# The gate ahead of the prompt's attention in a hybrid decoder layer: score banks, a pool for probabilities, and the planned order

## The chip, the core and the metric

The kernel runs on one core of one Trainium2 chip. It is one launch; what counts is device time in microseconds (us), the median of several executions. The core has a matrix engine (TensorE, PE in the rows), three engines for elementwise work (VectorE or DVE, ScalarE or ACT, GpSimd or POOL), a queue on SyncE (SP) that issues every transfer of this kernel, an on-chip memory of 128 partitions (SBUF) and eight accumulator banks (PSUM) into which TensorE writes. Each engine works through its own list of instructions in order and waits for the others by semaphores.

## What is computed

One inference step of one decoder layer, for a prompt of 512 tokens and for eight samples of one token with 2,048 tokens of past each, which lie in pages of 128 tokens. The part of the reference around which the change works, shortened:

```python
kc = _compress(ck, pk, w1k, w2k); vc = _compress(cv, pv, w1v, w2v)   # gelu(blocks @ w1) @ w2
s = einsum('bqgrd,bkgd->bgrqk', q, kc) * ATTN_SCALE                   # compressed branch
p = _masked_softmax(s, cmp_end <= q_pos); o_c = einsum(p, vc)
...                                                                   # importance -> top 16 blocks
s = einsum('bqgrd,bgqnd->bgrqn', q_rot, ks) * ATTN_SCALE              # selected branch
p = _masked_softmax(s, kmask); o_s = einsum(p, vs)
s = einsum('bqgrd,bkgd->bgrqk', q_rot, kw) * ATTN_SCALE               # window branch
p = _masked_softmax(s, wm); o_w = einsum(p, vw)
o = gate0 * o_c + gate1 * o_s + gate2 * o_w
...
s = einsum('bqhmd,bkhmd->bhmqk', qb, dk) * ATTN_SCALE                 # differential attention
p = softmax(where(k_pos <= q_pos, s, -inf)); o = einsum(p, dv)
o = rmsnorm(o[..., 0, :] - lam * o[..., 1, :], subln_g)
```

The same is done for the prompt (all keys are its own) and for each sample (keys from the pages). Then come the output projection, a gated feed-forward network with a short convolution, and the last norm.

## The kernel before, in words

The program has four parts in time: the input projection (to about 180 us), the compression of the samples' pages (to about 320 us), attention (to about 480 us), and the output projection and the feed-forward network (to the end). From the projection on to the first products of the output projection, the order is not written by hand. Small generators (`p_...`) yield one operation at a time with the events (`E(...)`) that it needs and sets; class `Issue` plays them against each other with planned times, picks the next one for each engine and emits the instructions in that order. The kernel is built 69 times: eight rehearsals, each planned from the latest starts of the one before it, then 60 variants with random shifts of the best plan, and last the build with the plan that ended first. So a change to one generator can move instructions anywhere in this part, and a time that the planner reckons with is not a time of the chip.

The generators that matter here:

- `p_product` multiplies the split pages of sample `b` with the compression's weights `w1`, first the keys (`k`), then the values (`v`): 24 products (three for each of eight steps) for each of 32 units in `cunits`. The sums of one sample and kind share a bank of `ACC`, a ring of four banks; `p_post` takes it from there (gelu, then the products named `hy,w2p` for keys and `w2v,hy` for values).
- `p_scores` and `p_window` collect the sample's scores against the selected pages and the window in banks 6 and 7 (`Ss`, `Sw`; products `cp,Qzs` and `qu,Qzs`).
- `p_nsa(b2)` (L1563) is the softmax of those scores for four samples. VectorE finds maxima, TensorE transposes them (`cst,nsc`, L1584), VectorE reduces, TensorE transposes back (`cst,m`, L1597), VectorE copies, ScalarE does three exponentials, VectorE adds, TensorE sums (`nsc,cst`), VectorE takes the reciprocal and scales `Ss`, TensorE transposes it (`cst,Ss`, L1628) and `Sw` (`cst,Sw`, L1639).
- `p_v` is the sample's product of probabilities with the pages of values: `vp,Sd` and `vp,Ss`, two pages for each load, eight and four matmuls. `p_vload` issues the 64 loads into a ring `VS` of six buffers. A buffer comes free after the `vp,Ss` of its pair of loads.
- `p_qk(i)` is the score step of unit `i` of the prompt (12 units: 4 heads' rows times the branches selected, window and differential). In the order each unit makes three packs for each of two groups: query blocks 0 and 1 (128 and 256 keys), block 2 (384) and block 3 (512), named `z,q` or `z,dq`. A pack needs a bank of `SR`, a ring of four. `p_exp` empties it: VectorE's masked minimum (L1835, `CUSTOM_DVE_ANT_0` in the rows), then ScalarE's exponential into a tile `p0` to `p3`. `p_scale` divides by the sums, `p_turn` transposes the probabilities (L1896), `p_pv` multiplies with the values.
- `p_switch` closes the pools of the compression: the event `right` comes when the pages are split and scored and the last key products are done, and opens the pools `W0` and `VR` (for the vp loads); `left` comes when everything that uses pool `C1` is done, and opens pool `AT` (for the prompt's tiles).
- `p_main` (L2243) runs all units' `p_qk` in a row.

In the kernel before, `p_main` waits for `left`, for `Sw` and `Ss` to be out of their banks, and for the last accumulator of the values; the banks of the roles are fixed: scores in 0, 1, 7 and 2, outputs in 3.

Of the kernel before, what the change touches and what calls it, by code (L numbers as in the profile page):

```python
# [20 lines left out]
B = 8  # L21
# [208 lines left out]
class Slot:  # L230


    def __init__(self, ring):
        self.ring, self.got, self.done = ring, Event(), Event()
        n = len(ring.slots)
        self.needs = [ring.slots[n - ring.size].done] if n >= ring.size else []
        if n:
            self.needs.append(ring.slots[n - 1].got)
        ring.slots.append(self)


class Ring:
    def __init__(self, size):
        self.size, self.slots = size, []
# [176 lines left out]
def _build(tc, T, plan, last):  # L421
# [838 lines left out]
    def p_product():  # L1260
        yield E("w", 23)
        yield E("w", 24)
        for n, (b, kv, sh) in enumerate(cunits):
# [10 lines left out]
            for i in range(2):  # L1274
                wh, wl = w1[kv, i]
                for s in range(4):
# [11 lines left out]
                    sets = [asl] if first else []  # L1288
                    if (i, s) == (1, 3):
                        sets += [wsl.done, E("prod", n)]  # L1290
# [452 lines left out]
    def p_switch():  # L1743
# [6 lines left out]
        def f():  # L1750
            RAW[1].close()
            RAW[0].close()
            Q0.close()
            PL["W0"] = Pool(tc, "W0", side="right")
            PL["VR"] = Pool(tc, "VR", side="right")
            pcs.append(PL["W0"]("wo", [128, 1024], F32, 3).rearrange("p (a b) -> p a b", b=512))
# [65 lines left out]
    def p_exp(i, g, qs, box, sl, wslot):  # L1822
# [4 lines left out]
        for q in qs:  # L1827
# [4 lines left out]
            def f():  # L1832
                if q == 0 and g == 0:
                    W[i] = at("w", [128, 6, 4], F32, 4)
                ve.tensor_tensor_reduce(out=x, in0=x, in1=cm[:, S - n:], scale=-SC, scalar=3e38, op0=OP.add, op1=OP.min,  # L1835
                                        accum_out=W[i][:, g, q:q + 1])
            yield (("dve", tdve(n), f, PS),) + ((wslot,) if first and q == 0 else ())
        for q in qs:
# [4 lines left out]
            def f():  # L1843
                t = at(f"p{q}", [128, n], F32, NPR[q])
                act(t, xs[q], AF.Exp, bias=W[i][:, g, q:q + 1], scale=-1.0, accum_out=W[i][:, 2 + g, q:q + 1])
                PB[i, g, q] = t, pr
# [33 lines left out]
    def p_turn(i):  # L1880
        br, r, gs = units[i]
        for c in range(3):
# [242 lines left out]
    def p_half(b, vb, sl):  # L2125
# [3 lines left out]
        b2, b4 = b // 4, b % 4  # L2129

# [112 lines left out]
    def p_main():  # L2243
        for e in (E("left"), E("Sw"), E("Ss", 1)):
            yield e
        yield cacc["v", B - 1].done
# [5 lines left out]
        Q.spawn(p_out(2, 1, OR, "o"), 7, Q.now)  # L2252

# [11 lines left out]
    for f, prio in ((p_stage2(), 0), (p_load(), 0), (p_w1v(), 0), (p_split(), 1), (p_product(), 3), (p_group("k"), 2), (p_group("v"), 2), (p_scores(), 2), (p_wload(), -1), (p_window(), 1),  # L2265
                    (p_turned(), 5), (p_vn(), 5), (p_nsa(0), 1), (p_nsa(1), 1), (p_cmp_sample(0), 1),
                    (p_cmp_sample(1), 1), (p_switch(), 0), (p_outs(), -3),
                    (p_vload(), 0), (p_win(), -1), (p_main(), 3),
# [11 lines left out]
    W0, VR = PL["W0"], PL["VR"]  # L2280
    PL["AT"].close()
# [23 lines left out]
    def wout():  # L2305
# [19 lines left out]
        ROLE["acc"], turn["acc"] = (1, 0, 2, 3), 0  # L2325
# [36 lines left out]
    ROLE["acc"], turn["acc"] = (0, 1, 2, 3, 6, 7), 4  # L2362
# [213 lines left out]
```

## Time and profile before

| | |
|---|---|
| median of 3 runs | 923.12 us (922.76 to 923.97) |
| the profiled execution | 923.06 us, span 921.2 us |
| TensorE busy | 899.1 us of the span (98%), 8,628 matmul records |
| VectorE / ScalarE / GpSimd busy | 573.5 / 384.4 / 168.3 us |
| transfers | 179.83 MB, mean 195 GB/s |
| granted TensorE clock, mean | 0.99 of full speed |

All times in the rows are us from the start of the span. A row of the order of time gives the start, the time from the first start to the last end, the engine, the line of the kernel (many operations come from a helper and have its line, L426 for matmuls), the operation, output<-inputs, sizes, how many instructions are merged in it, and in brackets how long the engine was idle before it and what ended that. A product in fp32 shows as two matmul records, so a row has twice the instructions of the order's listing. The end of a matmul is modelled.

### The profile page before, as it was taken

Reading aid. Unit: us, or ns where it says so; the run is one execution under the profiler, and the core shown is the slowest. Engines: PE = TensorE matmul, PEld = TensorE weight load, DVE = VectorE, ACT = ScalarE, POOL = GpSimd, SP = SyncE. Lnnn points to the kernel's source line nnn. Section 1 sums busy time; section 2 is a strip of 40 time slices with the busy share of each in tenths; the row PEclk is TensorE's granted clock in tenths of the full one; section 3 lists DMA queues with packets and bytes.
Section 4 is the critical chain, followed back from the end, with each engine's and each line's share of the span. In section 5 each row is a group of like instructions: output and inputs, shape, how many; then the busy total and the mean of one; then the engine's idle time right before and its main releaser. Section 6 shows DMA issues by size and latency. Waiting matters only on the chain.

```text
span 921.2 us, 22310 instructions
## 1 busy us (share of the span) xinstructions
PE 899.1 (98%) x8628; PEld 805.7 (87%) x8628; DVE 573.5 (62%) x1362; ACT 384.4 (42%) x790; POOL 168.3 (18%) x342
## 2 busy tenths in 40 slices
PE   8999999999999999999998999999999999999996
PEld 5998888889999856656578999999999999999995
DVE  7697563365768696768854667777777777311233
ACT  5256331254555564565652234444444444211120
POOL 5221110000111100101113442111112121224230
PEclk9999999989999999999999999999999999999998
DMA  7749999997777599898733522222222222433322
GB/s 265 241 145 369 347 361 354 320 297 240 227 244 229 207 372 376 291 338 286 246 123 134 150 95 102 92 93 92 93 92 93 92 93 63 151 105 119 104 76 94
DMA packets 86060, 179.83 MB, mean 195 GB/s; under 512 B 10049, under 2 KB 28994, under 8 KB 85954
## 3 DMA queue, kind: packets, MB, share of 16 engines
q1 hardware_dynamic: 85954, 178.41, 56.4%
q8 instruction: 68, 1.11, 0.5%
q14 instruction: 38, 0.31, 0.1%
HBM read 165.78 MB, written 12.59 MB: 194 GB/s over the span
## 4 chain that ended last, share of the span: by engine, by line
PE 89%; DMA 4%; DVE 3%; issue 2%; SPq 1%; ACT 1%; POOL 0%; POOLq 0%; DVEq 0%
PE bank L426 85%; PE bank L1896 3%; DMA kp<-in_kpg 2%; SPq L527 1%; DMA kcT<-vn 1%; DVE bank L1835 1%; DMA cp<-in_cpg 1%; DMA wr<-in_w_in 0%; PE bank L557 0%; DMA vp<-in_vpg 0%; DVE y L438 0%; PE bank L1707 0%; DVE wl L435 0%; ACT gh L429 0%; ACT xh L429 0%
## 5 line engine op out<-in xcount | busy, mean ns | idle before, releaser
L426 PE MATMUL bank<-gl,wh 128*128 128x260 f32 x704 | 199.0, 283 | 0.0
L426 PE MATMUL bank<-gh,wl 128*128 128x260 f32 x704 | 198.9, 283 | 0.0
L426 PE MATMUL bank<-gh,wh 128*128 128x260 f32 x704 | 198.9, 282 | 0.0
L429 ACT ACTIVATE wh<-wr 128x1024 fp32r<-128x1024 f32 (+2 forms) x94 | 96.9, 1030 | 190.2 <-PE bank L426 162.8
L435 DVE TENSOR_TENSOR wl<-wr,wh 128x1024 fp32r<-128x1024 f32 (+1 forms) x86 | 111.2, 1293 | 95.9 <-ACT wh L429 95.5
L426 PEld LDWEIGHTS bank<-gh,wh 128*128 128x128 f32 x704 | 132.6, 188 | 0.0
L426 PEld LDWEIGHTS bank<-gl,wh 128*128 128x128 f32 x704 | 132.5, 188 | 0.0
L426 PEld LDWEIGHTS bank<-gh,wl 128*128 128x128 f32 x704 | 132.4, 188 | 0.0
L426 PE MATMUL bank<-xh,wh 128*128 128x260 f32 (+1 forms) x368 | 105.5, 289 | 1.1 <-ACT wh L429 1.1
L426 PE MATMUL bank<-xl,wh 128*128 128x260 f32 (+1 forms) x368 | 104.5, 286 | 1.8 <-DVE xl L438 1.7
L426 PE MATMUL bank<-xh,wl 128*128 128x260 f32 x352 | 100.1, 284 | 0.0
L426 PE MATMUL bank<-hh,wh 128*128 128x260 f32 (+2 forms) x340 | 96.3, 283 | 0.0
L426 PE MATMUL bank<-hh,wl 128*128 128x260 f32 (+2 forms) x340 | 96.1, 283 | 0.0
L426 PE MATMUL bank<-hl,wh 128*128 128x260 f32 (+2 forms) x340 | 96.0, 282 | 0.0
L426 PEld LDWEIGHTS bank<-xh,wh 128*128 128x128 f32 (+1 forms) x368 | 68.9, 187 | 6.8 <-issue 4.5
L438 DVE SCALAR_TENSOR_TENSOR c<-u,cvw,c 128x536 f32<-128x536 f32 x88 | 69.6, 791 | 2.8 <-ACT c L429 1.3
L426 PEld LDWEIGHTS bank<-xl,wh 128*128 128x128 f32 (+1 forms) x368 | 68.9, 187 | 2.6 <-DVE xl L438 2.5
L426 PEld LDWEIGHTS bank<-xh,wl 128*128 128x128 f32 x352 | 66.9, 190 | 0.0
L426 PEld LDWEIGHTS bank<-hh,wl 128*128 128x128 f32 x340 | 64.1, 188 | 0.0
L426 PEld LDWEIGHTS bank<-hh,wh 128*128 128x128 f32 x340 | 64.0, 188 | 0.0
L441 DVE TENSOR_TENSOR u<-bank,rst 128x260 f32<-128x260 f32 x132 | 40.0, 333 | 38.6 <-PE bank L426 33.0
L426 PEld LDWEIGHTS bank<-hl,wh 128*128 128x128 f32 x340 | 64.0, 188 | 0.0
(392 smaller groups left out, 1913.3 us busy)
## 6 DMA issues: line engine op xcount, KB each, us to landing
vp<-in_vpg SPq DMA_DIRECT2D x128, 320.0 KB, 5.5
kp<-in_kpg SPq DMA_DIRECT2D x128, 256.0 KB, 5.4
cp<-in_cpg SPq DMA_DIRECT2D x128, 192.0 KB, 3.9
wr<-in_w_up SPq DMA_DIRECT2D x44, 512.0 KB, 3.2
wr<-in_w_in SPq DMA_DIRECT2D x21, 512.0 KB, 5.5
wr<-in_w_down SPq DMA_DIRECT2D x16, 512.0 KB, 3.4
out_zT<-z SPq DMA_DIRECT2D x14, 260.0 KB, 5.5
wr<-in_w_down SPq DMA_DIRECT2D x8, 384.0 KB, 3.1
```

The lines of the kernel that those rows point to most:

```text
L426: te.matmul(out, l, r, start=start, stop=stop)
L429: se.activation(out=out, in_=in_, func=func, **kw)
L435: eng.tensor_tensor(out=out, in0=a, in1=b, op=OP.subtract)
L438: ve.scalar_tensor_tensor(out=out, in0=a, scalar=s, in1=b, op0=o0, op1=o1, **kw)
L441: eng.tensor_tensor(out=out, in0=a, in1=b, op=op)
L527: sy.dma_start(out=dst, in_=src[bass.ds(numbers[k][i - k], 1)].rearrange("o p f -> (o p) f"))
L1835: ve.tensor_tensor_reduce(out=x, in0=x, in1=cm[:, S - n:], scale=-SC, scalar=3e38, op0=OP.add, op1=OP.min, accum_out=W[i][:, g, q:q + 1])
L1896: te.transpose(p[:, j * 128:(j + 1) * 128], PB[i, g, q][0][:, k * 128:(k + 1) * 128], ident)
```

## The change

It does five things. Probabilities `p0` to `p3` and their sums `w` get a pool of their own, `PA`, opened at `right` instead of lying in `AT`, which opens at `left`. `p_main` waits for `right` and for the first product of the last unit pair (`last product`) instead of `left`, `Sw`, `Ss` and the last accumulator. The first four score slots and the first output slot each wait for their own bank: three score banks and the output bank are the last four accumulator banks of the compression, in the order in which these fall free; the fourth, bank 7, has an event of its own (`bank7`, from the new `p_bank7`). `p_turn` and `p_half`, whose tiles still lie in `AT`, wait for `left` themselves. And the output projection takes its banks in the order that goes with the new roles. All that computes is unchanged. The core of the diff:

```diff
@@ class Slot
-        self.needs = [ring.slots[n - ring.size].done] if n >= ring.size else []
+        self.needs = [ring.slots[n - ring.size].done] if n >= ring.size else list(ring.first[n:n + 1])
@@ class Ring
-        self.size, self.slots = size, []
+        self.size, self.slots, self.first = size, [], []
@@ p_product
                     sets = [asl] if first else []
+                    if first and n == len(cunits) - 2:
+                        sets.append(E("last product"))
@@ p_switch
             PL["VR"] = Pool(tc, "VR", side="right")
+            PL["PA"] = Pool(tc, "PA", side="right")
@@ p_exp
-                    W[i] = at("w", [128, 6, 4], F32, 4)
+                    W[i] = PL["PA"]("w", [128, 6, 4], F32, 4)
-                t = at(f"p{q}", [128, n], F32, NPR[q])
+                t = PL["PA"](f"p{q}", [128, n], F32, NPR[q])
@@ p_turn
+        if i == 0:
+            yield E("left")
@@ p_half
+        yield E("left")
@@ p_main
-        for e in (E("left"), E("Sw"), E("Ss", 1)):
+        for e in (E("right"), E("last product")):
             yield e
-        yield cacc["v", B - 1].done
+        k = [ROLE["acc"][(len(ACC.slots) + j) % 4] for j in range(4)]
+        ROLE["s"], ROLE["o"], ROLE["out"] = (k[0], k[1], 7, k[2]), (k[3],), (k[1], k[0], k[2], k[3])
+        a = [sl.done for sl in ACC.slots[-4:]]
+        SR.first.extend((a[0], a[1], E("bank7"), a[2]))
+        OR.first.append(a[3])
...
+    def p_bank7():
+        yield E("Sw")
+        yield E("Ss", 1)
+        yield (None, 0.0, lambda: None), E("bank7")
@@ _build
-                    (p_vload(), 0), (p_win(), -1), (p_main(), 3),
+                    (p_vload(), 0), (p_win(), -1), (p_main(), 3), (p_bank7(), 3),
...
+    PL["PA"].close()
...
-        ROLE["acc"], turn["acc"] = (1, 0, 2, 3), 0
+        ROLE["acc"], turn["acc"] = ROLE["out"], 0
...
-    ROLE["acc"], turn["acc"] = (0, 1, 2, 3, 6, 7), 4
+    ROLE["acc"], turn["acc"] = ROLE["out"] + (6, 7), 4
```

What it does to the order, at three places. The lists leave out what only waits. Lines differ by one to ten between the two kernels.

First place, TensorE, the first `p_nsa`. Before: from its sums (`nsc,cst`) on, between the last products of the compression (`wh`, `wl` with `w1v`); its `cst,Ss` comes two rows after the last one here.

```order
L426 MATMUL bank_4887<-nsc,cst 128x2
L426 MATMUL bank_4766<-wh,w1vh_2654 128x256
L426 MATMUL bank_4766<-wl,w1vh_2654 128x256
L426 MATMUL bank_4766<-wh,w1vl_2655 128x256
L1707 MATMUL bank_4896<-cst,z_94 128x128 x4
L1738 MATMUL bank_4904<-cst,Pc 128x128 x4
L426 MATMUL bank_4766<-wh,w1vh_2654 128x256
L426 MATMUL bank_4766<-wl,w1vh_2654 128x256
L426 MATMUL bank_4766<-wh,w1vl_2655 128x256
L426 MATMUL bank_4917<-w2v,hy 128x64 x2
L426 MATMUL bank_4766<-wh,w1vh_2656 128x256
L426 MATMUL bank_4766<-wl,w1vh_2656 128x256
```

Now: the last 21 products, `cst,nsc` and the first four score products come directly ahead of the first row here.

```order
L427 MATMUL bank_4937<-z_91,q_73 128x384
L427 MATMUL bank_4938<-z_91,q_73 128x384
L1600 MATMUL bank_4946<-cst,m_2646 128x2
L427 MATMUL bank_4948<-hy,w2p 128x128 x2
L427 MATMUL bank_4955<-w2v,hy 128x64 x2
L1710 MATMUL bank_4969<-cst,z_99 128x128 x4
L427 MATMUL bank_4978<-kcT,Qzc 32x128 x4
L427 MATMUL bank_4991<-nsc,cst 128x2
L1631 MATMUL bank_5014<-cst,Ss 128x128 x4
L427 MATMUL bank_5020<-z_91,q_73 128x512
L427 MATMUL bank_5021<-z_91,q_73 128x512
```

The steps of `p_nsa` have moved behind the last product, and the first pack of scores (blocks 0 to 2 of unit 0) stands ahead of `cst,m`; nothing stands between `nsc,cst` and `cst,Ss`.

Second place, VectorE, between the copy of `nsc` and the addition ahead of the sums, in the same `p_nsa`. Before:

```order
L1599 COPY nsc<-bank_4805 128x2
L441 TENSOR_TENSOR hy<-hy,hx 128x256
L435 TENSOR_TENSOR wl<-cp,wh 128x32x8
L1446 TENSOR_REDUCE sm<-s_4486 128x8
L1447 TENSOR_SCALAR sm<-sm 128x8
L1448 RECIPROCAL sm<-sm 128x8
L441 TENSOR_TENSOR sm<-sm,gN 128x8
L441 TENSOR_TENSOR nsc<-nsc,Sn 128x1
L1616 RECIPROCAL nsc<-bank_4887 128x2
```

Now (the copy of `nsc` is the row ahead of these; `ISA` is the masked minimum of a score block, with its readout):

```order
L1839 ISA bank_4927,w<-bank_4927,cm 128x128
L1839 ISA w 128x1
L1839 ISA bank_4928,w<-bank_4928,cm 128x128
L1839 ISA w 128x1
L1839 ISA bank_4928,w<-bank_4928,cm 128x256
L1839 ISA w 128x1
L1839 ISA bank_4927,w<-bank_4927,cm 128x256
L1839 ISA w 128x1
L1839 ISA bank_4937,w<-bank_4937,cm 128x384
L1839 ISA w 128x1
L1717 COPY dv<-bank_4969 128x512
L442 TENSOR_TENSOR nsc<-nsc,Sn 128x1
```

Five score blocks and the copy of `dv` (values of the differential branch) have come ahead of the addition.

Third place, TensorE, the first vp products of the samples. Before:

```order
L426 MATMUL bank_4967<-vc,PTc 32x128
L426 MATMUL bank_4967<-vp,Sd 32x128 x16
L426 MATMUL bank_4967<-vp,Ss 32x128 x4
L426 MATMUL bank_4967<-vp,Sd 32x128 x8
L426 MATMUL bank_4766<-wh,w1vh_2656 128x256
L426 MATMUL bank_4766<-wl,w1vh_2656 128x256
L426 MATMUL bank_4766<-wh,w1vl_2657 128x256
L426 MATMUL bank_4967<-vp,Sd 32x128 x8
L426 MATMUL bank_4967<-vp,Ss 32x128 x4
L426 MATMUL bank_5034<-ce,cst 32x128
L1490 MATMUL bank_5034<-cst,ce 128x32
L426 MATMUL bank_5038<-z_91,q_73 128x128
```

Now:

```order
L427 MATMUL bank_5061<-vc,PTc 32x128
L427 MATMUL bank_5061<-vp,Sd 32x128 x16
L427 MATMUL bank_5061<-vp,Ss 32x128 x4
L427 MATMUL bank_5061<-vp,Sd 32x128 x16
L427 MATMUL bank_5061<-vp,Ss 32x128 x4
L427 MATMUL bank_5061<-vp,Sd 32x128 x16
L427 MATMUL bank_5061<-vp,Ss 32x128 x4
L427 MATMUL bank_5142<-z_93,q_73 128x384
L427 MATMUL bank_5143<-z_93,q_73 128x384
L1587 MATMUL bank_5150<-cst,nsc 2x128
L427 MATMUL bank_5061<-vp,Sd 32x128 x8
L1600 MATMUL bank_5200<-cst,m_2646 128x2
```

Before, four loads are followed by the score steps, and loads 4 to 6 come between those; now six loads (48 `vp,Sd`) follow each other without a step in between.

## Rows read from the trace of the kernel before

**Rows 1.** The page's first part, busy time (us, share, instructions).

```profile
PE 899.1 (98%) x8628; PEld 805.7 (87%) x8628; DVE 573.5 (62%) x1362; ACT 384.4 (42%) x790; POOL 168.3 (18%) x342
```

**Rows 2.** By stage: window, its length, engines' busy us, clock, DMA share, GB/s.

```profile
308.00:336.00 28.00, 25.94 (x364) 20.03 (x362) 21.29 (x91) 15.92 (x50) 2.86 (x6) 1.00 0.88 313
336.00:484.00 148.00, 146.27 (x1847) 90.81 (x1847) 108.15 (x371) 85.99 (x255) 14.02 (x14) 1.00 0.81 284
```

**Rows 3.** TensorE in order of time: start, us, instruction, [idle before, releaser].

```profile
322.60 1.57 PE L426 MATMUL bank<-z,q 64*128 64x128 f32 x12
...
326.55 0.42 PE L426 MATMUL bank<-vp,Sd 128*32 128x128 f32 x8 [0.17 <-DMA vp<-in_vpg]
327.36 0.43 PE L426 MATMUL bank<-vp,Sd 128*32 128x128 f32 x8 [0.39 <-DMA vp<-in_vpg]
328.90 1.13 PE L426 MATMUL bank<-z,q 64*128 64x512 f32 x4 [1.11 <-ACT p L429]
```

**Rows 4.** TensorE's steps of the first p_nsa, beside the last products.

```profile
309.20 0.27 PE L1584 MATMUL bank<-cst,nsc 128*2 128x128 f32 x1
...
310.55 0.19 PE L1597 MATMUL bank<-cst,m 2*128 2x2 f32 x1 [0.34 <-DVE m L1590]
...
312.72 0.38 PE L426 MATMUL bank<-nsc,cst 128*128 128x2 f32 x2
...
315.67 0.60 PE L1628 MATMUL bank<-cst,Ss 128*128 128x128 f32 x4
```

**Rows 5.** TensorE, four hy products and what follows them.

```profile
316.96 0.71 PE L426 MATMUL bank<-hy,w2p 128*128 128x128 f32 x4
317.43 0.37 PE L426 MATMUL bank<-wh,w1vh 128*128 128x256 f32 x1
```

**Rows 6.** VectorE's steps of the same p_nsa, in order of time.

```profile
310.77 0.16 DVE L1599 COPY nsc<-bank 128x2 f32<-128x2 f32 x1 [0.37 <-PE bank L1597]
...
312.52 0.15 DVE L441 TENSOR_TENSOR nsc<-nsc,Sn 128x1 f32<-128x1 f32 x1
313.14 0.17 DVE L1616 RECIPROCAL nsc<-bank 128x2 f32<-128x2 f32 x1 [0.48 <-PE bank L426]
...
313.62 0.28 DVE L444 TENSOR_SCALAR Sw<-Sw,nsc 128x128 f32<-128x128 f32 x1
...
314.15 0.48 DVE L444 TENSOR_SCALAR Ss<-Ss,nsc 128x512 f32<-128x512 f32 x1
```

**Rows 7.** ScalarE, the first of its exponentials in the same p_nsa.

```profile
310.97 0.72 ACT L429 ACTIVATE Ss<-Ss,nsc 128x512 f32<-128x512 f32 x1 [1.23 <-DVE nsc L1599]
```

**Rows 8.** VectorE, masked minima of the first scores, and a 512-wide copy.

```profile
325.36 0.29 DVE L1835 CUSTOM_DVE_ANT_0 bank<-bank,cm 128x128 f32<-128x128 f32 x1
...
325.74 0.43 DVE L1835 CUSTOM_DVE_ANT_0 bank<-bank,cm 128x256 f32<-128x256 f32 x1
...
329.47 0.56 DVE L1835 CUSTOM_DVE_ANT_0 bank<-bank,cm 128x384 f32<-128x384 f32 x1
...
336.95 0.68 DVE L1910 COPY pt<-bank 128x512 f32<-128x512 f32 x1
```

**Rows 9.** DMA of vp: all landings; windows 430-434, 385-388.5, 319-325.

```profile
DMA to landing us min/median/max: 2.8/5.5/7.9
...
vp<-in_vpg SPq DMA_DIRECT2D x3, 320.0 KB, 3.5
...
vp<-in_vpg SPq DMA_DIRECT2D x4, 320.0 KB, 4.9
...
DMA packets 1101, 2.39 MB, mean 399 GB/s; under 512 B 148, under 2 KB 148, under 8 KB 1100
```

**Rows 10.** By stage, as rows 2, around the lower clock at 188 us.

```profile
184.00:188.00 4.00, 2.83 (x21) 2.19 (x21) 0.43 (x1) 2.50 (x6) 0.00 (x0) 0.86 0.90 278
188.00:192.00 4.00, 4.00 (x17) 2.85 (x17) 3.47 (x10) 2.88 (x10) 0.00 (x0) 0.50 1.05 393
192.00:196.00 4.00, 4.00 (x30) 4.00 (x29) 2.64 (x6) 2.67 (x7) 0.62 (x4) 0.79 0.95 309
```

## The prediction

> **What bounds the kernel now.** I read the page first: TensorE is busy for 899.1 us of the span [rows 1], so at most some 22 us of waiting can be won in the whole program. Then the table by stage: from 308 to 336 us, where the compression's products end and the prompt's attention begins, 2.06 us of 28 are idle, from 336 to 484 us only 1.73 of 148 [rows 2]. So the stage that the change touches is bound by TensorE, with one small hole at its head. TensorE's own rows name it: 0.17 and 0.39 us for pages of vp, then 1.11 us for ScalarE's probabilities before the two 512-wide scores [rows 3], and 0.34 us before the maxima's second transpose [rows 4]. All this is start-up: four score banks fill, the softmax of the first unit has not begun to drain them, and the vp pages have only just been asked for.
>
> The instructions are the same before and after, 7,203 matmuls on TensorE in both. So the new time is the old one, less the waits that go, plus those that come, plus what another mix of neighbours costs.
>
> **What goes.** The idle 2.06 us at 308 to 336 [rows 2]. A recorded end is modelled: four hy products are given 0.71 us from 316.96, yet the next product starts at 317.43 [rows 5], so about 0.2 us of each wait hides under the row before it. With four waits that is 0.8 us more: 2.8 us to win here, 2.06 at the least. The 1.73 us of the later attention I leave where it is.
>
> **What the order does not do.** In the listing the first score product stands behind the last compression product, not among the products: the search let it wait. What did move is the sample's first softmax, p_nsa(0). Before, its six TensorE steps stood between products; now they stand after them, with only the scores and a few small steps as cover. And the sample's vp products now begin with six loads in one piece.
>
> **What comes, 1: p_nsa(0) without cover.** Before, its chain ran like this: maxima transposed at 309.20, back at 310.55, sums at 312.72, scaled scores transposed at 315.67 [rows 4]. Now there are three places to look at.
>
> (a) From cst,nsc to cst,m the chain took 1.35 us [rows 4]. Now the first six score instructions lie between, a row of 1.57 us from 322.60 [rows 3]. Covered: 0.
>
> (b) From cst,m to the sums (nsc,cst) TensorE now has hy, w2v, cst,z and kcT: 0.47 us for hy (316.96 to 317.43) [rows 5], about as much for each of the other three, and some switching: an estimate of 2.2 us. VectorE copies nsc 0.22 us after cst,m (310.55, 310.77) [rows 4, 6]. Behind that copy there now stand five masked minima and the copy of dv ahead of the one small add that the sums wait for. Two of 128 take 0.38 each by their starts (325.36, 325.74), two of 256 take 0.43, one of 384 takes 0.56 and a 512-wide copy 0.68 [rows 8]: 2.9 us, 2.8 with some overlap. The add itself is followed by the sums 0.20 us later (312.52, 312.72) [rows 4, 6]. So the sums stand 0.22 + 2.8 + 0.2, that is 3.2 us after cst,m where TensorE is there after 2.2: 1.0 us of waiting. At the least it is 0: ScalarE's exponentials alone had the add ready 1.75 us after the copy [rows 6, 7], 2.2 us after cst,m with the sums. I take 1.0 because VectorE works its queue in order.
>
> (c) From the sums to the transposes of Ss nothing stands in between now: row follows row. The transposes need the reciprocal (0.42 us after the sums), three small steps to 313.62, and the scaling of Ss at 0.48 us, with Sw's scaling and a reduction of cf ahead of it [rows 4, 6]. Without what else VectorE had in between, that is 0.42 + 0.48 (313.14 to 313.62) + 0.48, and an estimated 0.2 each for Sw and cf: 1.8 us, and a hand-over of 0.1. TensorE is there after 0.3: it waits 1.6 us. This can't vanish: no other instruction can step in. At the least 1.3.
>
> Then the two 512-wide scores need the banks of the first pack, whose last exponential now waits behind one that needs cf: 0.4 us, between 0 and 0.7. Sum of 1: 3.0 us, from 1.3 to 3.3.
>
> **What comes, 2: six loads in one piece.** The loads are asked for when the right side is free, now some 15 us ahead of their use, so the first six are there and rows 3's 0.17 and 0.39 go. But TensorE eats them in 3.3 us. Load 6 gets its buffer after the first pair, 1.1 us in, and is wanted at 4.5 us. Its two pages land 3.5 us after issue when the queue was empty, and at 399 GB/s when it is full, 1.64 us for the 655 KB of a load [rows 9]. So: second page issued at 1.9, landed at 5.4, against 4.7 wanted: 0.7 us. Loads 7, 8 and 9 follow at 1.64 us each, wanted about 0.8, 1.0 and 1.4 us apart: 0.9, 0.6 and 0.3 us. That is 2.5 us; with the 2.8 us of the shortest landing [rows 9] it is 1.8. I take 2.2. At the least 0, if vp products that start 3 us late by the waits above find the queue faster than I think; at the most 3.9, with landings of 4.9 us as after 385 [rows 9], 1.4 us slower.
>
> [...]
>
> **What comes, 3: the neighbours.** Between the first product and the first up-projection TensorE changes its kind of work 376 times instead of 372. Even at 0.27 us, a whole small transpose [rows 4], four changes are 1.1 us: I take 0, with 1.1 either way.
>
> **Moves that cost nothing.** Probabilities in a place of their own, and the new bank numbers: no instruction more. The waits that p_turn and p_half get (for the left side) end before their first use, since the sample's k product, on which the left side waits, now stands ahead of cst,z. SyncE's load of w_out into z now waits for the copy of dv and holds the four stores and kcT behind it, but load 6 is asked for some 7 us later: hidden by that; if not, each microsecond counts in full.
>
> **The sum.** 923.06 - 2.8 + 3.0 + 2.2 + 0 = 925.5 us for the profiled execution; the median is 0.06 higher, so 925.5 for it too.
>
> **Rivals.**
> A. The clock drops as well. [...] Against it: from 308 to 336, with 2.06 us idle, the clock stayed at 1.00 [rows 2]. [...]
> B. The DMA keeps up. All of the 2.2 us goes, and 3.0 - 2.8 stays: 923.3 us, no difference. For it: 15 us of lead. Against: landings of 5.5 us in the median [rows 9].
> C. The lead carries on. The first unit's softmax runs earlier against the rest; then the later waits, 1.73 us from 336 to 484 [rows 2], shrink too, and the DMA keeps up: 923.3 - 1.7 - 0.7 for the neighbours = 920.9 us. Faster. Against: place (c) stays in any case.
> The change not doing what it says (scores beside products) is no rival but the forecast's ground; the listing shows it.
>
> **How the numbers follow.** Forecast (slower by waits, clock unmoved) 0.40; A 0.20; B 0.24; C 0.16. Predicted time: 925.5. The forecast's own bounds are 923.06 - 2.8 + 1.3 + 1.8 - 1.1 = 922.3 and 923.06 - 2.06 + 3.3 + 3.9 + 1.1 = 929.3. The range goes from 921.2, which leaves out half of C, to 929.0, which leaves out the upper end of A. A difference of 0.2% (1.85 us) is about what a measurement of this kernel can tell from no change. Slower by more: most of the forecast (0.33) and A: 0.53. Within: B and the rest of the forecast: 0.32. Faster by more: C without its smallest gains: 0.15.
>
> **What would show it.** Right: in the new trace TensorE idles 1 us or more before nsc,cst and before cst,Ss, named after VectorE, right behind the last products, and 1 to 3 us in all before vp products that wait for DMA, 3 to 10 us after the first of them; the 1.11 us for p is gone. Wrong: idle time between the last product and the tenth vp load under 3 us; or the clock row under 9 there (A); or the stage from first vp to last PV with less than 1 us idle (C).

## The result, and the profile after

The changed kernel takes 927.91 us (median of 5 runs, 926.01 to 929.36); the kernel before, run beside it, 922.83 us. The ratio is 1.0051, with a 95% interval of 1.0037 to 1.0065: slower, by about 4.7 us. The time lies in the stated range, 2.4 us above the forecast and on 928.0, which is the forecast with the 2.5 us that I reckoned for rival A's drop of the clock. The profiled execution is the fastest of the five, 926.01 us with a span of 924.1.

The windows of the changed kernel answer to [rows 2, 10]; their columns are start and end, length, busy time of PE, PEld, DVE, ACT and POOL with the number of instructions, granted clock, DMA share and GB/s. TensorE is busy for 901.4 us in all, 899.1 before [rows 1]; the averages over the program do not show what happened.

```profile
308.00:336.00 28.00, 24.02 (x294) 16.95 (x291) 20.29 (x87) 14.42 (x52) 0.61 (x1) 0.84 0.77 270
336.00:484.00 148.00, 146.59 (x1882) 89.48 (x1876) 105.74 (x363) 82.52 (x243) 12.74 (x13) 1.00 0.82 294
```

```profile
184.00:188.00 4.00, 2.44 (x13) 1.14 (x13) 1.88 (x5) 1.98 (x6) 0.00 (x0) 0.89 0.96 341
188.00:192.00 4.00, 4.00 (x26) 4.00 (x25) 3.61 (x8) 3.48 (x8) 0.00 (x0) 0.69 1.04 365
192.00:196.00 4.00, 4.00 (x40) 3.76 (x39) 2.06 (x9) 2.10 (x7) 0.76 (x6) 1.00 0.99 327
...
316.00:320.00 4.00, 2.12 (x16) 1.68 (x16) 3.79 (x18) 2.63 (x14) 0.00 (x0) 1.00 0.98 362
320.00:324.00 4.00, 4.00 (x14) 1.71 (x13) 2.27 (x9) 2.05 (x7) 0.00 (x0) 0.53 0.72 274
324.00:328.00 4.00, 4.00 (x73) 3.17 (x73) 3.19 (x21) 2.44 (x8) 0.00 (x0) 0.62 0.01 2
...
332.00:336.00 4.00, 2.56 (x49) 1.80 (x50) 2.76 (x16) 3.62 (x15) 0.61 (x1) 0.73 0.94 313
336.00:340.00 4.00, 3.96 (x52) 2.30 (x44) 2.25 (x11) 1.46 (x6) 0.00 (x0) 0.84 1.00 363
```

In what follows, the joint is the stretch where the compression's last products and the first scores and vp products meet, some 308 to 340 us. From 308 to 336 us TensorE is idle for 3.98 us where it was 2.06 [rows 2], and the clock is 0.84 where it was 1.00. In slices of 1 us it falls to 0.50 of full speed twice: from 321 to 327 us, behind the idle time of 316 to 320, and from 334 to 337, behind that of 332 to 334. Counted over 300 to 355 us, which holds the whole joint in every run below, the idle time is 4.3 us against 2.7 before, and the clock row (0.91 over 55 us) is worth 5.0 us against none. Against that the lower clock at 184 to 196 us cost 1.7 us in this execution, 3.4 before [rows 10]. The later attention is as it was: 1.41 us of idle time in 336 to 484, 1.73 before [rows 2]. These terms alone (1.6 + 5.0 - 1.7) would make 4.9 us between the profiled executions, which differ by 2.95. Ahead of the joint and behind it TensorE was idle 1.1 us less in the first 184 us (busy 179.31 us of them, 178.22 before), 0.5 us more from 184 to 300 and 0.2 us less from 484 to 530, which leaves 4.1. The last 1.1 us are not resolved; some of the loss on the clock row falls on time in which TensorE waited anyway (from 334 to 335 us it was busy for 0.68 us at 0.50).

TensorE in order of time through the joint, changed kernel (columns as in [rows 3]):

```profile
314.64 0.22 PE L1600 MATMUL bank<-cst,m 2*128 2x2 f32 x1
314.79 0.71 PE L427 MATMUL bank<-hy,w2p 128*128 128x128 f32 x4
315.34 0.56 PE L427 MATMUL bank<-w2v,hy 128*128 128x64 f32 x4
316.12 0.65 PE L1710 MATMUL bank<-cst,z 128*128 128x128 f32 x4 [0.23 <-ACT kcT L430]
316.70 1.06 PE L427 MATMUL bank<-kcT,Qzc 128*32 128x128 f32 x8
317.75 0.35 PE L427 MATMUL bank<-nsc,cst 128*128 128x2 f32 x2
319.86 0.78 PE L1631 MATMUL bank<-cst,Ss 128*128 128x128 f32 x4 [1.75 <-DVE ce L1481]
320.57 2.08 PE L427 MATMUL bank<-z,q 64*128 64x512 f32 x4
...
325.64 0.43 PE L427 MATMUL bank<-vp,Sd 128*32 128x128 f32 x3
...
331.94 0.43 PE L427 MATMUL bank<-vp,Sd 128*32 128x128 f32 x8 [0.56 <-DMA vp<-in_vpg]
...
333.63 0.50 PE L427 MATMUL bank<-vp,Sd 128*32 128x128 f32 x8 [1.12 <-DMA vp<-in_vpg]
334.46 0.65 PE L427 MATMUL bank<-vp,Sd 128*32 128x128 f32 x8 [0.32 <-DMA vp<-in_vpg]
```

The two places of the prediction are there: 1.75 us before `cst,Ss`, 2.0 us in three pieces for vp. The 512-wide scores behind `cst,Ss` take 2.08 us, at 0.50 from 321 to 323 us, where four of them took 1.13 at 1.00 [rows 2, 3]: the lower clock. The 1.11 us for ScalarE's p [rows 3] is gone.

### The profile page after: what moved, and what is told of

Same layout as the page of the kernel before. It is cut to its first block, busy times and chain, and to the rows that moved or that the text cites. A ratio compares the mean times of both kernels' runs of the same rounds, so it can differ in the third digit from the quotient of the medians.

```text
span 924.1 us, 22288 instructions
## 1 busy us (share of the span) xinstructions
PE 901.4 (98%) x8628; PEld 807.0 (87%) x8628; DVE 572.3 (62%) x1363; ACT 383.7 (42%) x793; POOL 165.3 (18%) x338
## 3 DMA queue, kind: packets, MB, share of 16 engines
q8 instruction: 68, 1.11, 0.5%
## 4 chain that ended last, share of the span: by engine, by line
PE 91%; DVE 3%; DMA 3%; issue 1%; SPq 1%; ACT 1%; POOL 0%; POOLq 0%; DVEq 0%; ACTq 0%
PE bank L427 87%; PE bank L1902 3%; DMA vp<-in_vpg 2%; DMA cp<-in_cpg 1%; DMA kp<-in_xT 1%; DVE wl L436 1%; PE bank L558 0%; DVE z L442 0%; DVE y L439 0%; PE bank L1710 0%; ACT gh L430 0%; DVE sq L775 0%; DVE bank L1839 0%; ACT xh L430 0%; SPq L528 0%
## 5 line engine op out<-in xcount | busy, mean ns | idle before, releaser
L436 DVE TENSOR_TENSOR wl<-cp,wh 128x256 fp32r<-128x256 f32 x126 | 47.0, 430 | 27.3 <-ACT wh L430 23.1
```

Source lines behind the costliest of these rows:

```text
L436: eng.tensor_tensor(out=out, in0=a, in1=b, op=OP.subtract)
```

## The experiments

Theory 1 was: the loss is the first `p_nsa` without cover and the vp loads in one piece, and the waits there bring the clock down. Against it stood that the clock falls for the thin work of the joint whatever the waits, and that the loss belongs to the whole new order, of which the joint is only the place that was looked at. For each run the ratio is taken against the kernel before, run on the same chip beside it.

### e1: idle transposes before `cst,Ss`

```diff
             p = box["p"] = ps("m")
+            if b2 == 0:
+                for k in range(14):
+                    te.transpose(p[:, (k % 4) * 128:(k % 4 + 1) * 128], ident, ident)
             for k in range(4):
                 te.transpose(p[:, k * 128:(k + 1) * 128], Ss[:, b2, k * 128:(k + 1) * 128], ident)
```

> The changed kernel in its own order, with 14 transposes of the identity by itself put in front of the four transposes of Ss (cst,Ss) of the first p_nsa; they write the same bank, which the four then overwrite, so nothing of the result changes and 14 small matmuls are added. Changed kernel: 927.9 us (its profiled run 926.0), 1.75 us of idle before cst,Ss, granted clock 0.53 and 0.62 in 320 to 328 us. Theory 1, the idle time there brings the clock down: the 14 fit into the wait (some 0.11 us each), TensorE shows no idle before cst,Ss, the clock stays at 1.00 up to the waits for vp, and 2.5 to 3.4 us come back: 924.5 to 925.5 us. Rival, the thin work of the whole joint (small products, one after the other) brings the clock down whatever fills one gap: the clock drops as before and the time is 927.5 to 928.5 us.

928.25 us, ratio 1.0047 (1.0031 to 1.0062). TensorE in e1:

```profile
321.06 0.35 PE L427 MATMUL bank<-nsc,cst 128*128 128x2 f32 x2
323.10 1.94 PE L1632 MATMUL bank<-cst 128*128 128x128 f32 x14 [1.69 <-ACT ce L430]
324.84 1.06 PE L1634 MATMUL bank<-cst,Ss 128*128 128x128 f32 x4
325.83 2.08 PE L427 MATMUL bank<-z,q 64*128 64x512 f32 x4
```

The filling did not fill: the transposes of a constant, which need nothing from VectorE, waited 1.69 us themselves. What they need is the bank, one of two that all these small steps share, and it still held `kcT,Qzc`, the compressed scores of the second four samples, until ScalarE's exponential `ce` had read them. The clock fell as before (0.57 in 324 to 328 us), and as the wait was still empty, that decides nothing between theory 1 and its rival. But the run corrects the price of place (c): besides the scaling of Ss, which my sum used, there is a second cause that ends at the same moment. In the changed kernel's trace, VectorE and ScalarE:

```profile
317.45 0.15 DVE L442 TENSOR_TENSOR nsc<-nsc,Sn 128x1 f32<-128x1 f32 x1
...
319.23 0.49 DVE L445 TENSOR_SCALAR Ss<-Ss,nsc 128x512 f32<-128x512 f32 x1
319.77 0.06 DVE L1481 MEMSET ce<- 32x1 f32 x1
```

```profile
319.29 0.36 ACT L430 ACTIVATE ce<-bank,cf 32x127 f32<-32x127 f32 x1 [1.34 <-DVE cf L1475]
```

Ss is scaled at 319.72, the bank is read at 319.65. By these rows, taking away one alone would have gained less than 0.1 us.

### e5: the same filling, in a bank that is free

```diff
-            ve.reciprocal(out=f, in_=box["p"][:, 0:2])
+            p = box["p"]
+            ve.reciprocal(out=f, in_=p[:, 0:2])
+            if b2 == 0:
+                for k in range(12):
+                    te.transpose(p[:, 128 + (k % 3) * 128:256 + (k % 3) * 128], ident, ident)
```

> The changed kernel in its own order, once more with small transposes of the identity against the idle time before cst,Ss; in the first try they stood behind the wait itself, since the bank they shared with cst,Ss was not free. Now 12 of them write unused columns of the bank of the sums (nsc,cst), and wait only for the reciprocal to have read those, some 0.5 us after the sums. Changed kernel: 927.9 and, with the misplaced filling, 928.3 us. Theory 1, the idle time before cst,Ss brings the clock down: TensorE is idle for 0.3 to 0.5 us there instead of 1.7, the clock stays at 1.00 to the waits for vp, and the time is 925 to 926 us. Rival, the thin work of the joint as a whole brings it down: clock 0.5 to 0.6 in the 8 us behind the last product as before, 927.5 to 928.5 us.

925.08 us, ratio 1.0010 (0.9996 to 1.0024); that interval and the changed kernel's do not meet. TensorE, then windows, in e5:

```profile
319.40 0.35 PE L427 MATMUL bank<-nsc,cst 128*128 128x2 f32 x2
320.02 1.53 PE L1623 MATMUL bank<-cst 128*128 128x128 f32 x12 [0.26 <-DVE nsc L1620]
321.51 0.63 PE L1635 MATMUL bank<-cst,Ss 128*128 128x128 f32 x4
322.07 1.13 PE L427 MATMUL bank<-z,q 64*128 64x512 f32 x4
...
324.90 0.31 PE L427 MATMUL bank<-vp,Sd 128*32 128x128 f32 x3
```

```profile
320.00:324.00 4.00, 3.98 (x26) 2.64 (x26) 3.20 (x14) 2.74 (x9) 0.00 (x0) 1.00 0.96 352
324.00:328.00 4.00, 4.00 (x122) 3.63 (x125) 3.57 (x21) 2.45 (x8) 0.00 (x0) 1.00 0.20 50
...
332.00:336.00 4.00, 3.41 (x51) 2.19 (x51) 2.71 (x16) 3.86 (x16) 0.61 (x1) 0.57 0.92 307
```

`cst,Ss` comes 2.11 us after the sums, as in the changed kernel (317.75 to 319.86). The wait has not become shorter by anything; TensorE only had useless work in it. Yet the clock stays at 1.00 through 328 us, the 512-wide scores take 1.13 us again, and from `cst,Ss` to the first vp product it is 3.4 us instead of 5.8 (321.51 to 324.90; 319.86 to 325.64). That is 2.4 us for the first drop of the clock, in the profile; the ratios give 0.41%, 3.8 us, with both intervals' widths on it. The other executions agree: averaged over them, the granted clock of the whole program is 0.9868 in the changed kernel's five, 0.9875 in e1's ten and 0.9898 in e5's twelve, and the difference is worth 2 to 3 us of 925. With nothing else moved on TensorE, the lower clock (0.53 and 0.62 in 320 to 328 us without the filling, 1.00 in both slices with it) belonged to the empty wait ahead of it.

### e9: the second wait filled too

12 more such transposes in the second `p_nsa`, right behind VectorE's first reading of the maxima, where the changed kernel waits for vp.

```diff
             ve.tensor_copy(out=m4[:, 0:4], in_=m4[:, 4][:, None, :].to_broadcast([2, 4, 32]))
+            if b2 == 1:
+                p = box["p"]
+                for k in range(12):
+                    te.transpose(p[:, 128 + (k % 3) * 128:256 + (k % 3) * 128], ident, ident)
```

> As e5 (12 idle transposes between the sums and cst,Ss of the first p_nsa), and 12 more in the second p_nsa, behind VectorE's first reading of the transposed maxima, which is where TensorE waits for the vp loads 6 to 9. In e5 (925.1 us) the granted clock fell to 0.57 in 332 to 336 us, behind 1.1 us of waiting there; the changed kernel shows 0.73 and 0.84 there. Theory 1, each lower clock belongs to the wait just ahead of it: the clock stays at 1.00 there too, 1 to 1.7 us come back, 923.5 to 924.5 us. Rival, the second drop follows from the long run of small vp products and not from the wait, or the added transposes come in the way of the vp products: 925 to 927 us.

924.81 us, ratio 1.0020 (1.0009 to 1.0031): not to be told from e5. The windows of e9:

```profile
324.00:328.00 4.00, 4.00 (x129) 3.67 (x128) 3.57 (x21) 2.29 (x8) 0.00 (x0) 1.00 0.22 45
332.00:336.00 4.00, 3.24 (x62) 2.34 (x60) 2.66 (x16) 2.50 (x12) 0.61 (x1) 1.00 0.96 322
```

The clock now stays at 1.00 through the whole joint, as theory 1 says; but the time does not follow. The added row stands behind a wait of 1.26 us for vp, which it does not fill (331.24 is the wait's end, 331.59 the row's start). It takes 1.53 us, and the maxima's second transpose and the next vp products stand behind it: from the second `cst,nsc` to `kcT,Sw` it is 4.5 us (329.35 to 333.88); in e5, whose clock fell there, 4.2 us (329.64 to 333.87). So it cost at least what it saved. The clock did what theory 1 says, the time did not.

### e6: the wait put into the kernel before

```diff
+        def g():
+            if b2 == 0:
+                for k in range(6):
+                    ts(ve, Ss[:, b2], Ss[:, b2], 1.0)
+            ts(ve, Ss[:, b2], Ss[:, b2], f[:, 0:1])
-        yield ("dve", tdve2(512), lambda: ts(ve, Ss[:, b2], Ss[:, b2], f[:, 0:1])),
+        yield ("dve", tdve2(512), g),
```

> The kernel before, its order unchanged on TensorE, with six multiplications of Ss by 1.0 in front of VectorE's scaling of Ss in the first p_nsa: about 0.4 us each, 2.4 us. It makes a wait of the size that the change brought, in a kernel that has none there. Ss is then ready 1.4 us after TensorE asks for it, and hy, which stands behind it on VectorE, some 2.4 us late. Theory 1, such a wait costs itself and brings the clock down: 2 us of idle in 312 to 320 and a clock of 0.5 to 0.8 in the 8 us after it, 926.5 to 928.5 us. Rival, a wait of this size alone leaves the clock at 1.00: 925 to 926 us. Second rival, what is lost at the joint is won back in the later waits: 923 to 924 us.

927.81 us, ratio 1.0035 (1.0020 to 1.0049). TensorE, then windows, in e6:

```profile
319.13 0.63 PE L1634 MATMUL bank<-cst,Ss 128*128 128x128 f32 x4 [1.72 <-DVE Ss L444]
...
321.16 1.19 PE L426 MATMUL bank<-hy,w2p 128*128 128x128 f32 x4 [0.61 <-ACT Ss L429]
...
336.06 1.13 PE L426 MATMUL bank<-z,q 64*128 64x512 f32 x4 [2.33 <-ACT p L429]
```

```profile
316.00:320.00 4.00, 2.29 (x20) 1.95 (x18) 3.72 (x10) 1.06 (x3) 0.00 (x0) 1.00 0.96 314
320.00:324.00 4.00, 3.39 (x18) 3.08 (x17) 1.45 (x5) 1.46 (x4) 0.00 (x0) 0.59 1.04 408
324.00:328.00 4.00, 4.00 (x66) 3.34 (x64) 1.14 (x6) 0.45 (x2) 0.00 (x0) 0.56 0.30 113
```

The order, banks and gates are those of the kernel before; only a wait of the changed kernel's size was added, among products that are wide and dense. The clock falls behind it, to 0.59 and 0.56 in 320 to 328 us, and the time rises by 3 to 4 us. The idle time of 300 to 355 us rises by 3.0 us: 2.3 at the wait itself, and 1.2 before the 512-wide scores, where ScalarE's p is now waited for 2.33 us instead of 1.11 [rows 3], while the 0.56 us for vp [rows 3] are gone. So in this kernel such a wait, 1.72 us with nothing of the change, was enough to bring the clock down and to cost most of what the change cost (ratio 1.0035 of 1.0051). How much of these 3 to 4 us is the clock's and how much the idle time's, e6 does not tell.

### e2: the first `p_nsa` back among the products

```diff
-        yield ("pe", 0.46, g), sl
+        yield ("pe", 0.46, g), sl, E("SsT", b2)
@@ p_main
-        for e in (E("right"), E("last product")):
+        for e in (E("right"), E("last product"), E("SsT", 0)):
```

> The changed kernel, but p_main also waits until the first p_nsa has issued its cst,Ss; the planner then puts the whole of that softmax among the last products, as in the kernel before, and the first scores right behind cst,Ss. The banks, the pool for probabilities and the early gate stay. Theory 1, the loss is the first p_nsa without cover and the lower clock after it: no idle of 0.5 us or more before nsc,cst and cst,Ss, clock 1.00 over the joint as long as vp waits stay under 1.5 us together, 922 to 924 us. Rival, the loss is the order that the new gate brings everywhere, or the new banks and pool, and p_nsa only the place where it shows: 926 to 929 us with other waits in its place.

928.26 us, ratio 1.0043 (1.0028 to 1.0058). Theory 1 falls here as a whole account. `cst,Ss` now follows the last product without idle time, and the clock is 1.00 to 332 us. But the planner laid another order, and that has waits of its own: 0.47 and 0.66 us before `cst,nsc` and `cst,m`, 0.66 us for ScalarE's p, and the clock falls behind the last one, to 0.63 and 0.51 in 332 to 340 us. The later attention, too, has 3.6 us of idle time in 340 to 484 (140.45 busy of 144; the kernel before, 1.6). Whether that comes of the gate or of the draw of the plan, e2 does not tell. TensorE, then windows, in e2:

```profile
332.42 2.88 PE L427 MATMUL bank<-z,q 64*128 64x512 f32 x4 [0.66 <-ACT p L430]
```

```profile
332.00:336.00 4.00, 3.58 (x8) 1.57 (x9) 3.57 (x19) 2.77 (x9) 1.51 (x2) 0.63 1.04 404
336.00:340.00 4.00, 4.00 (x13) 1.35 (x11) 3.66 (x15) 3.55 (x10) 0.00 (x0) 0.51 0.94 356
340.00:484.00 144.00, 140.45 (x1866) 88.64 (x1865) 103.83 (x352) 81.57 (x238) 11.78 (x11) 1.00 0.80 283
```

### e4: the pool alone

The old gate and the old banks, and of the change only the pool `PA`; the order is that of the kernel before on every engine.

```diff
@@ p_main (of the changed kernel)
-        for e in (E("right"), E("last product")):
+        for e in (E("left"), E("Sw"), E("Ss", 1)):
             yield e
...
-        SR.first.extend((a[0], a[1], E("bank7"), a[2]))
-        OR.first.append(a[3])
+        yield cacc["v", B - 1].done
```

> One part of the change alone: the pool for probabilities and sums, opened with the vp pool, but p_main with its old gate and the old banks. Its order on TensorE is that of the kernel before, row for row. Theory 1 (only the order matters): 922.8 us, within 0.6 us of the kernel before. Rival (another place of p0 to p3 in memory, or the waits for the left side, cost by themselves): 924.5 us or more.

923.95 us, ratio 0.9999 (0.9983 to 1.0014). The place of the probabilities costs nothing that can be measured here, to within some 0.15%.

### e7 and e8: other draws of the plan

Both kernels, planned with another start value of the random shifts.

```diff
-    rng = np.random.default_rng(0)
+    rng = np.random.default_rng(1)
```

> The changed kernel, planned with another start value of the random shifts (1 instead of 0): the same generators, gates, banks and pools, another order. Its first p_nsa again ends with cst,Ss straight behind nsc,cst after the last product, and six vp loads again come in one piece; cst,nsc stands two steps of products earlier. Theory 1, those two places make the loss, and the planner makes them in every draw: 1.5 us or more of idle before cst,Ss, 1.5 to 2.5 us at vp, a lower clock behind them, 926.5 to 929 us. Rival, the loss is this one draw's: anything from 920 to 925 us with the same two places in it.

> The kernel before, planned with another start value of the random shifts (the values 1 and 2 give the same order). The first p_nsa stands among products as in the kernel before; but six vp loads come in one piece as in the changed kernel. So it has one of the two places without the other. Theory 1: no idle before cst,Ss, 1.5 to 2.5 us of waiting for vp, clock at 1.00 or a short dip: 924 to 926.5 us. Rival, the draws differ by more than the gate does: under 922 or over 927 us.

The changed kernel: 926.86 us, ratio 1.0037 (1.0022 to 1.0053), with 1.68 us of idle time before `cst,Ss`, 2.7 us for vp, and a clock of 0.50 in 324 to 328. The two places come in this draw too. But the kernel before, with its other draw, takes 929.68 us, ratio 1.0050 (1.0034 to 1.0067): the rival's side. Nothing of the change is in it, and it loses as much as the change did, at yet other places: in 340 to 484 us TensorE is idle for 7.3 us, where the kernel before has 1.6. The profiled execution is the slowest of its eight (936.57 us), so its waits are larger than those of the median. From e8's list of waits (in total, times, longest):

```profile
PE bank L426 <- DMA vp<-in_vpg: 4.1, 5, 1.7
PE bank L426 <- DMA cp<-in_cpg: 2.8, 4, 1.5
PE bank L426 <- DMA kcT<-vn: 2.8, 2, 2.3
```

### e3, e10 and e11: the scores beside the products

What the change makes possible and the planner did not do, made by hand.

```diff
-        return self.plan.get((p["name"], p["k"]), t) + (self.STICK * self.turn(p) if o[0] == "pe" else 0.0)
+        return (self.plan.get((p["name"], p["k"]), t) + (self.STICK * self.turn(p) if o[0] == "pe" else 0.0)
+                - (20.0 if p["gen"].__name__ == "p_main" and p["k"] < 6 else 0.0))
```

> The changed kernel with 20 us of urgency given to the first six score steps, so that the planner does what the change makes possible: the scores of the first unit's blocks 0 to 2 stand some 10 products before the last one, and the first p_nsa's steps between products again; only nsc,cst to cst,Ss still has little in between (three products and four transposes). Theory 1: some 1 us of idle before cst,Ss instead of 1.75, six vp loads in a piece again with 1 to 2 us of waiting, a dip of the clock at one of the two places at the most: 924 to 926.5 us. Rival, scores beside products are worth what the change wants (softmax of the first unit runs ahead): the later waits go too and the time is 920.5 to 922.5 us. Second rival, the order is worse whatever is moved: 927 to 929 us.

918.48 us, ratio 0.9943 (0.9920 to 0.9965): faster than both kernels, and beyond what theory 1 gave. The first scores stand at 309.73, 10 us ahead of the last product. TensorE, then windows, in e3:

```profile
321.13 0.66 PE L1632 MATMUL bank<-cst,Ss 128*128 128x128 f32 x4 [0.34 <-DVE Ss L446]
```

```profile
308.00:340.00 32.00, 31.12 (x408) 21.32 (x402) 27.06 (x116) 21.88 (x67) 0.00 (x0) 1.00 0.91 322
340.00:484.00 144.00, 142.35 (x1829) 89.50 (x1828) 104.39 (x357) 82.17 (x245) 9.71 (x8) 1.00 0.83 293
484.00:530.00 46.00, 44.68 (x373) 44.47 (x372) 26.84 (x30) 11.78 (x15) 21.06 (x17) 1.00 0.44 140
```

Against the kernel before, 1.4 us of idle time are gone in 308 to 340 (0.9 left of 2.2) and 1.5 us in 484 to 530 (1.3 of 2.8); 340 to 484 is as it was. So the lead did not carry through the attention, as the rival says, but the joint is smooth and the clock stays at 1.00 from 308 to 340 us. Is that the scores' place or the draw? The same with start values 1 and 2:

> The kernel of e3 (the changed one with the first six score steps made urgent), planned with start value 1 of the random shifts instead of 0. The first unit's scores stand some 5 to 10 products ahead of the last one again; cst,Ss has one step (cst,z) between it and nsc,cst, and six vp loads come in one piece. e3 took 918.5 us, the changed kernel planned with value 1 took 926.9 us. Theory A, the scores beside the products make the gain: some 5 to 8 us under the changed kernel of the same draw, 918.5 to 922 us. Rival, e3's gain was the luck of its draw: 924 to 928 us.

> The same with start value 2. Here the two 384-wide scores and two small steps stand between nsc,cst and cst,Ss, so that wait should be under 0.5 us; six vp loads come in one piece. Theory A: 917.5 to 921 us. Rival, e3's gain was the luck of its draw: 923 to 928 us.

926.07 us, ratio 1.0031 (1.0019 to 1.0044), and 924.94 us, ratio 1.0022 (1.0009 to 1.0035). The rival holds. The gain of 5 to 8 us over the changed kernel of the same draw did not come: e10 cannot be told from e7 (1.0037). In e10 the joint is as smooth as in e3 (1.6 us of idle time in 300 to 355, clock 1.00), and the time is lost ahead of it: 3.0 us more idle time than in e3 in the first 60 us, with 3.7 us in one piece for ScalarE's dq, and 2.1 us more in 184 to 300. In e11 a new wait of 1.24 us for VectorE's `tr` has opened in the joint, with a lower clock behind it (0.77 and 0.81 in 328 to 336 us).

### e12: a filled wait elsewhere

The kernel of e3 (918.48 us) in its own order, and five products of the identity by itself (ten records, 1.2 us by estimate) among the group's narrow products (`phk,w1h` and `phk,w1l`, 132 and 66 columns), in the gap before the compression's first products, where e3 (at 185.2 us), the changed kernel and the kernel before wait 1.05 to 1.16 us for pages of cp and the clock then falls: in 188 to 196 us it is 0.50 and 0.70 in e3, 0.69 and 1.00 in the changed kernel, 0.50 and 0.79 in the kernel before [rows 10]. The five write columns of the group's bank that nobody reads.

```diff
                     mm(box["p"][:, :66], wl[:, q], x[:, q, 0, c], False, i + q == 8)
+                    if (kv, i, q) == ("k", 1, 6):
+                        for k in range(5):
+                            mm(box["p"][:, 256 + k % 2 * 128:384 + k % 2 * 128], ident, ident, False, False)
```

> [...] Theory 1, a filled wait keeps the clock: 1.00 or nearly so from 184 to 196 us, 2 to 3.5 us come back, 915 to 916.5 us. Rival, the clock falls there whatever stands in the gap, since the group's products are narrow, or the products take their 1.2 us from the wait's end: 918 to 920 us.

916.45 us, ratio 0.9926 (0.9903 to 0.9948). That is 2.0 us less than e3, but the two intervals overlap, and the runs are of two chips: the gain in time is likely, not shown. That the clock came back is shown: averaged over all executions, the granted clock of the whole program is 0.9927 in e3's six and 0.9953 in e12's six, worth 2.4 us. The windows of e12, where e3 has 0.95, 0.50 and 0.70:

```profile
184.00:188.00 4.00, 3.13 (x20) 1.74 (x19) 2.31 (x7) 2.43 (x6) 0.00 (x0) 1.00 1.00 368
188.00:192.00 4.00, 4.00 (x35) 4.00 (x35) 3.25 (x11) 4.00 (x9) 0.14 (x2) 1.00 0.98 329
192.00:196.00 4.00, 4.00 (x45) 3.52 (x44) 3.22 (x10) 3.88 (x13) 0.13 (x2) 1.00 0.92 295
```

All runs in one view. Idle time and clock loss are TensorE's from 300 to 355 us of the profiled execution (55 us less the busy time; 55 us times one minus the granted clock). The ratio is that of all executions; the profiled ones of e1 and e8 are the slowest of theirs:

| run | ratio | idle us | clock loss us |
|---|---|---|---|
| before | 1 | 2.7 | 0 |
| changed | 1.0051 | 4.3 | 5.0 |
| e1, filling behind the bank | 1.0047 | 4.2 | 5.0 |
| e2, p_nsa among products | 1.0043 | 2.2 | 3.3 |
| e3, scores early | 0.9943 | 1.7 | 0 |
| e4, pool alone | 0.9999 | 2.7 | 0 |
| e5, first wait filled | 1.0010 | 3.0 | 1.7 |
| e6, wait added to before | 1.0035 | 5.7 | 3.3 |
| e7, changed, draw 1 | 1.0037 | 4.7 | 5.0 |
| e8, before, draw 1 | 1.0050 | 2.6 | 1.7 |
| e9, both waits filled | 1.0020 | 2.8 | 0 |
| e10, scores early, draw 1 | 1.0031 | 1.6 | 0 |
| e11, scores early, draw 2 | 1.0022 | 3.1 | 1.7 |
| e12, e3 and a filled wait | 0.9926 | 1.2 | 0 |

Among runs with one order the two columns mostly go with the ratio: before, e4 and e6; changed, e1 and e5. They do not from e5 to e9, where 1.7 us of clock came back and the ratio did not fall. Between orders (e2, e8, e10) they do not, since other parts differ as well.

## Why the prediction was right, and where it was off

**What the order does not do.** Right: the scores stand behind the last product, and what moved is `p_nsa(0)`.

**(a)** Covered, as forecast: `cst,m` at 314.64 follows the scores without idle time.

**(b)** From `cst,m` to the sums it is 3.11 us (314.64 to 317.75), 3.2 forecast, and by the forecast way: VectorE's addition waited behind five minima and the copy of dv, and ended at 317.60. What was off is the look of it: the rows between were thought to need 2.2 us, and name 0.23 us of idle time, before `cst,z`, instead of 1.0. The rest lies under rows whose ends are modelled (1.06 us for `kcT,Qzc`).

**(c)** 2.11 us from the sums to `cst,Ss`, 1.75 of them idle; forecast 1.9 and 1.6. Right in size and place, but e1 showed a second cause that I had not looked for, the bank. The 0.4 us before the 512-wide scores did not come.

**Loads.** 2.0 us for vp, 2.2 forecast. They fall on loads 6 and 7 alone (0.56, 1.12, 0.32), not on 6 to 9. What makes them is the ring of six buffers, as the sum had it for load 6, and not the speed of the transfers: in 324 to 328 us the queue moves 2 GB/s, while SyncE waits 6.1 us for the first pair's buffer and asks for load 6 at 327.84.

**What goes.** The 1.11 us and the other start-up waits went, as forecast.

**The clock.** This is the step that failed. The forecast held the clock unmoved and gave rival A a chance of 0.20, since the kernel before had 2.06 us of idle time at this place at 1.00 [rows 2]. It fell, twice, for 5.0 us of loss on the windows; the page's clock row shows 8 in the slice from 323 to 346 us, which the prediction had named as a sign of being wrong. That the clock drops with the new waits was right, as e5 (1.00 with the wait filled) and e6 (0.59 and 0.56 behind a wait added) show. A's price of 2.5 us was my estimate, part of the 3.4 us that the lower clock lost at 184 to 196 us [rows 10]; it was about that of the first drop alone in the trace (2.4). With that drop taken out, 0.10% is left over the kernel before in e5 and 0.20% in e9, of 0.51%: the drop is most of the loss, and the waits, which were the whole forecast, the smaller part. The idle time itself rose by 1.6 to 1.9 us, forecast 2.4. So A should have been the likeliest case. That the median came out on A's 928.0 is in part luck: its waits were too large, its clock too cheap, and in the profile 2.8 us came back ahead of the joint (1.7 of clock at 184 to 196 us, 1.1 of idle time before), which no sum had. The range held because it was wide enough for A.

**What the prediction did not ask.** It took the order as given, and there it was right. But e7, e8, e10 and e11 show that the search's draw moves a kernel by up to 0.9% (the changed one by 0.14%, which is within the noise), as much as the change or more. That the gate, the banks or the pool as such make this kernel slower is not shown: the kernel before in another draw is as slow, and the gate with the scores made urgent has been faster once and slower twice. With one to three draws of each, the worth of the gate itself stays open.

## What to carry to other kernels

Here a wait of TensorE of 1.75 us cost its length and, as the clock fell behind it, more than that again (2.4 us, by e5's trace). A few useless products in the wait gave 2.4 to 3.8 us back in e5, and likely 2 in e12. They gave nothing that could be told in e1 (1.0047 against 1.0051), where they needed the bank that the wait was for, and in e9's second wait (1.0020 against e5's 1.0010), where they held up what could have gone on. Where a planner with random shifts lays the order, a change to its rules is also a new draw: plan both kernels with several start values before calling the difference the change's. Before a stall is priced by one chain, look at what else its instruction needs, the bank it writes above all.

## What the runs showed of the hardware

Idle time alone did not tell when the clock falls. 1.11 us of waiting left it at 1.00 in the kernel before [rows 3], where 0.66 us in e2 was followed by 0.63 and 0.51, in e9 1.3 us of waiting with the filling behind it left it up, and in e6 even 2.33 us before the 512-wide scores did (1.00 in 332 to 340). What the rows do show is that the same wait of 2.1 us, in the same order, was followed by a clock of 0.53 and 0.62 in 320 to 328 us when it was empty (the changed kernel) and of 1.00 in the same slices when twelve transposes of a constant stood in it (e5).

The cost of the drop in time was not the loss on the clock row: for the first drop the row lost 3.4 us (0.53 and 0.62 in 320 to 328 us), and the way from `cst,Ss` to the first vp product was 2.4 us longer. In e9 the row regains 1.7 us against e5, and the added row of 1.53 us takes it again.
